# A gated four-branch block: branch gates computed ahead of the mixers' projections, as seven half-size products per pair of column blocks

## The chip, the core and the metric

The kernel runs on one core of a Trainium2 chip. The metric is the device time of one execution in microseconds (us); a kernel's time is the median of its runs.

## The reference, cut to what matters

One layer, T = 1024 tokens, D = 1024 channels, all in float32. The part that the change concerns:

```python
h = rms_norm(x, norm_mix_g) * (1 + sc1) + sh1
p = h @ w_in                                   # mixers' columns, then 4 * D gate columns
y_a, y_b, y_c, y_d = rwkv7(...), spatial_gating(...), short_conv(...), s5(...)
# each mixer ends with  o @ w_out : 256 -> 1024; s5 has a second, sigmoid half
gates = sigmoid(p[..., OFF_G:]).reshape(T, 4, D)
merged = gates[0] * y_a + gates[1] * y_b + gates[2] * y_c + gates[3] * y_d
x = x + gt1 * (merged @ w_o)
h2 = rms_norm(x, norm_ffn_g) * (1 + sc2) + sh2
x = x + gt2 * (square(relu(h2 @ ffn_w1)) @ ffn_w2)
return rms_norm(x, final_g)
```

## The kernel before, in words

Every float32 operand of a large product is split into a rounded high part (`hi`, type fp32r, a cast on ACT) and a remainder (`lo`, a subtraction on DVE); both stand in `split`, lines 72 and 73. One product of a 128-row piece is three matmuls, hi·hi, hi·lo and lo·hi, into one PSUM bank (`mm3`, line 112). Each call of `mm3` is a **beat**: it also lets a background generator advance (`step`), which puts the small work of the S5, spatial-gating and RWKV mixers between the large products, after a given number of beats. RWKV is in three parts: `rwkv_1` prepares chunks, `rwkv_2` solves 32-row triangular blocks on DVE alone (lines 1051 and 1053), and `rwkv_3` is a serial recurrence over chunks on PE, ACT and DVE. `mods` sums the conditioning vector's products on DVE (lines 310 and 312) in the same background.

Activations are kept transposed: `hh[k]` and `hl[k]`, k = 0..7, are 128 channels by 1024 tokens. The order of the large work is: a, b and conv columns of `w_in`, then `gates(br)` for the branches 3 (S5), 1, 2 and 0 (RWKV), then `w_o`, then the feed-forward part. `gates(br)` runs over eight column blocks j and two token halves hf. For each it makes the gate, 8 beats over the 8 channel blocks (`h_mm`), then the mixer's projection, 2 beats (4 for S5); ACT takes the sigmoid out of PSUM (L1222), DVE multiplies projection and gate (L1236), POOL adds into `merged` (L1239, L1233 for S5); for the last branch DVE adds (L1241) and splits the sum for `w_o` (L72, L73). Weights come from `weight_queue`: `take` keeps `depth` = 2 prepared operands ahead, tiles `raw`, `whi` and `wlo` with two buffers each. Loads, stores and their waits stand in one SP queue, in order. The tile framework's scheduler then orders each engine's instructions, so that rows of neighbouring steps interleave.

```python
for hf in range(2):
    pg = self.h_mm(w, hf)
    nc.scalar.activation(sg, pg, AF.Sigmoid)
    ...
    v.tensor_tensor(m if first else sg, py[0], sg, op=ALU.mult)
```

Names: `pmm` are four PSUM banks for large products; `m`, `n`, `ev`, `sig`, `g2` (shown as `g`) are float32 tiles of 128x512; `wyr`, `wyh`, `wyl` are a projection's weights raw and split; `MX` in DRAM holds the mixers' outputs. The feed-forward part's first product (`up_queue`, `ffn_up`) is already made in seven products instead of eight.

Of the kernel before, what the change touches and what calls it, by code (L numbers as in the profile page):

```python
# [10 lines left out]
F32 = mybir.dt.float32  # L11
# [29 lines left out]
class Kern:  # L41
# [49 lines left out]

    def behind_next(self):

        es = ExitStack()
        if self.ahead:
            w = self.ahead[0]
            for ins in self.tail[id((w[0] if len(w) == 3 else w)[0])]:
                es.enter_context(self.tc.issue_after(ins))
        return es
# [755 lines left out]
    def conv(self):  # L855
# [322 lines left out]

    def wy_load(self, br, name, j):
# [18 lines left out]
        return w, hi, lo

    def gates(self, br, first, last):  # L1200

        nc, v = self.nc, self.nc.vector
        glu = br == 3
        ne = 2 if glu else 1
        if not first:
            self.flush()
        mx = [[None] * 2 for _ in range(2)]
        for hf in range(2):
            for r in range(2):
                raw = self.ev()  # L1210
                nc.sync.dma_start(raw, self.MX[br, r, :, hf * HALF : hf * HALF + HALF])
                hi, lo = self.g(dt=F32R, tag="n"), self.g(dt=F32R, tag="n")
                self.split(hi, lo, raw)
                mx[hf][r] = (hi, lo)
        for j in range(8):
            w, wyh, wyl = self.take()
            for hf in range(2):
                pg = self.h_mm(w, hf)
                sg = self.sg()
                pin = self.behind_next if hf else ExitStack  # L1220
                with pin():
                    nc.scalar.activation(sg, pg, AF.Sigmoid)  # L1222
# [458 lines left out]
    def weight_queue(self):  # L1681
# [206 lines left out]
```

## Time and profile before

| what | value |
|---|---|
| median of 3 runs | 1697.05 us (1696.71 to 1697.99) |
| the profiled execution's own time | 1698.43 us |
| its span, first to last instruction | 1696.7 us |
| granted TensorE clock, mean | 0.987 |
| PE busy / DVE / ACT / POOL | 1613.8 / 1004.0 / 652.4 / 631.0 us |
| moved by DMA | 234.68 MB, 138 GB/s over the span |

PE is the matmul engine, DVE the vector engine, ACT the scalar engine, POOL GpSimd, SP the queue that issues most DMAs. Busy time is the union of an engine's instructions; matmuls overlap in the record, so their durations (about 400 ns) are not their pace. An instruction's duration includes what it waits for inside the engine. L numbers are lines of the kernel before.

### The profile page before, as it was taken

Reading aid. Unit: us, or ns where it says so; the run is one execution under the profiler, and the core shown is the slowest. Engines: PE = TensorE matmul, PEld = TensorE weight load, DVE = VectorE, ACT = ScalarE, POOL = GpSimd, SP = SyncE. Lnnn points to the kernel's source line nnn. Section 1 sums busy time; section 2 is a strip of 40 time slices with the busy share of each in tenths; the row PEclk is TensorE's granted clock in tenths of the full one; section 3 lists DMA queues with packets and bytes.
Section 4 is the critical chain, followed back from the end, with each engine's and each line's share of the span. In section 5 each row is a group of like instructions: output and inputs, shape, how many; then the busy total and the mean of one; then the engine's idle time right before and its main releaser. Section 6 shows DMA issues by size and latency. Waiting matters only on the chain.

```text
span 1696.7 us, 22664 instructions
## 1 busy us (share of the span) xinstructions
PE 1613.8 (95%) x8083; PEld 1293.7 (76%) x8083; DVE 1004.0 (59%) x1729; ACT 652.4 (38%) x1206; POOL 631.0 (37%) x505
## 2 busy tenths in 40 slices
PE   3999999999999999999999998799999999999996
PEld 2798778777777777777888876588888878888875
DVE  5673545666538824233433567865555469669986
ACT  4522124556522112211222245544455446444343
POOL 2260223112220223222101374576556565128662
PEclk9999999999999999999999999799999999999998
DMA  8423136777675345331211446354444485562332
GB/s 276 131 63 66 52 118 195 180 188 175 143 151 182 63 138 174 107 116 35 75 48 62 170 146 172 92 178 150 154 157 141 161 309 170 161 223 87 99 125 99
DMA packets 262723, 234.68 MB, mean 138 GB/s; under 512 B 79351, under 2 KB 194282, under 8 KB 262610
## 3 DMA queue, kind: packets, MB, share of 16 engines
q1 hardware_dynamic: 254002, 224.83, 44.2%
q10 hardware_dynamic: 8464, 8.01, 1.9%
q8 instruction: 64, 1.05, 0.3%
q0 software_dynamic: 144, 0.39, 0.1%
q14 instruction: 49, 0.40, 0.1%
HBM read 172.59 MB, written 60.58 MB: 137 GB/s over the span
## 4 chain that ended last, share of the span: by engine, by line
PE 37%; DVE 8%; DMA 2%; issue 2%; ACT 2%; POOL 1%; POOLq 0%; DVEq 0%; ACTq 0%; SPq 0%
PE pmm L112 22%; PE pax L112 8%; PE pch L112 7%; DVE g L73 2%; DVE xx L73 1%; DMA raw<-in_ffn_w_dram 1%; DVE m L1523 1%; DMA raw<-FA 1%; DMA w<-in_ffn_w_dram 1%; ACT g L72 1%; DVE wlo L73 0%; POOL ev L1513 0%; DVE m L1526 0%; DVE m L1328 0%; DVE n L73 0%
## 5 line engine op out<-in xcount | busy, mean ns | idle before, releaser
L112 PE MATMUL pmm<-hh,whi 128*128 128x512 f32 x704 | 285.3, 407 | 3.9 <-ACT hh L410 3.9
L112 PE MATMUL pmm<-hl,whi 128*128 128x512 f32 x704 | 278.7, 396 | 5.3 <-POOL hl L412 4.1
L112 PE MATMUL pmm<-hh,wlo 128*128 128x512 f32 x704 | 278.3, 395 | 0.0
L73 DVE TENSOR_TENSOR wlo<-raw,whi 128x512 fp32r<-128x512 f32 (+1 forms) x140 | 105.8, 793 | 129.4 <-ACT whi L72 126.1
L112 PEld LDWEIGHTS pmm<-hh,whi 128*128 128x128 f32 x704 | 132.6, 189 | 34.7 <-ACT hh L410 5.1
L112 PEld LDWEIGHTS pmm<-hl,whi 128*128 128x128 f32 x704 | 133.2, 189 | 33.6 <-POOL hl L412 4.5
L112 PEld LDWEIGHTS pmm<-hh,wlo 128*128 128x128 f32 x704 | 133.2, 189 | 29.7 <-issue 0.9
L72 ACT CAST whi<-raw 128x512 fp32r<-128x512 f32 (+1 forms) x140 | 79.0, 612 | 158.2 <-PE pmm L112 141.5
L112 PE MATMUL pmm<-g,g 128*128 128x512 f32 x456 | 107.3, 390 | 0.6 <-DVE xx L1425 0.6
L112 PE MATMUL pmm<-n,wyh 128*128 128x512 f32 x320 | 106.3, 411 | 0.8 <-ACT n L72 0.8
L73 DVE TENSOR_TENSOR g<-raw,g 128x512 fp32r<-128x512 f32 x75 | 72.0, 959 | 48.7 <-ACT g L72 42.6
L112 PEld LDWEIGHTS pmm<-g,g 128*128 128x128 f32 x456 | 85.6, 188 | 18.9 <-DVE xx L1425 1.0
L1239 POOL TENSOR_TENSOR m<-m,sig 128x512 f32<-128x512 f32 x32 | 45.1, 1409 | 129.9 <-DVE sig L1236 129.8
L1222 ACT ACTIVATE sig<-pmm 128x512 f32<-128x512 f32 x64 | 38.1, 596 | 142.6 <-PE pmm L112 131.4
L84 POOL TENSOR_TENSOR raw<-raw,gt 128x1024 f32<-128x1024 f32 x16 | 39.1, 2444 | 136.3 <-DMA raw<-in_w_o_dram 131.6
L112 PE MATMUL pmm<-g,m 128*128 128x512 f32 x256 | 82.5, 404 | 3.4 <-ACT m L72 3.4
L1236 DVE TENSOR_TENSOR sig<-pmm,sig 128x512 f32<-128x512 f32 x48 | 32.9, 686 | 69.0 <-PE pmm L112 68.9
L72 ACT CAST g<-raw 128x512 fp32r<-128x512 f32 x75 | 46.5, 620 | 69.8 <-PE pmm L112 34.6
L112 PEld LDWEIGHTS pmm<-n,wyh 128*128 128x128 f32 x320 | 60.5, 193 | 16.4 <-issue 1.2
L73 DVE TENSOR_TENSOR n<-xx,m 128x512 fp32r<-128x512 f32 x64 | 54.9, 863 | 28.4 <-ACT m L72 28.3
L72 ACT CAST m<-xx 128x512 fp32r<-128x512 f32 x64 | 39.3, 620 | 75.8 <-PE pch L112 27.4
L112 PE MATMUL pch<-g,g 128*128 128x512 f32 x222 | 59.7, 402 | 8.7 <-DVE g L73 5.7
(480 smaller groups left out, 3833.3 us busy)
## 6 DMA issues: line engine op xcount, KB each, us to landing
raw<-FA SPq DMA_DIRECT2D x56, 512.0 KB
raw<-in_w_in_dram SPq DMA_DIRECT2D x52, 512.0 KB
FA<-xx SPq DMA_DIRECT2D x80, 256.0 KB
raw<-in_ffn_w_dram SPq DMA_DIRECT2D x36, 512.0 KB
mod<-in_ada_w_dram SPq DMA_DIRECT2D x64, 256.0 KB
w<-in_ffn_w_dram SPq DMA_DIRECT2D x32, 512.0 KB
raw<-in_w_o_dram SPq DMA_DIRECT2D x16, 512.0 KB
FA<-ev SPq DMA_DIRECT2D x32, 256.0 KB
```

Of the source, the lines that this page charges most:

```text
L72: a = nc.scalar.copy(hi, src)
L73: b = (eng or nc.vector).tensor_tensor(lo, src, hi.bitcast(F32), op=ALU.subtract)
L84: nc.gpsimd.tensor_tensor(raw, raw, scale, op=ALU.mult)
L112: mm = lambda *x, **y: self.nc.tensor.matmul(*x, **y, skip_group_check=open_)
L1222: nc.scalar.activation(sg, pg, AF.Sigmoid)
L1236: v.tensor_tensor(m if first else sg, py[0], sg, op=ALU.mult)
L1239: nc.gpsimd.tensor_tensor(m, m, sg, op=ALU.add)
L1523: v.tensor_tensor(dst, x, y, op=ALU.add)
```

## The change

The gates of all branches are made first, in `gates()`, for pairs of column blocks. A pair's 256 columns by 1024 channels, and h as 1024 channels by 1024 tokens, are cut in two by two, and the pair takes seven products of halves (4 beats each) instead of eight (Winograd's form of Strassen's scheme). `h_sums` and `h_blocks` make the three sums of h's quarters that the scheme needs, beside and behind the conv columns; `gate_queue` makes the weights' sums on POOL in place in the raw tiles and splits each operand; depth is 3. Products 1, 6, 7 and 4 of a pair accumulate in one bank, 5 and 3 in another; between them ACT copies a bank out or DVE adds the earlier copy to it. The sigmoids go to a DRAM tensor `G` (64 stores of 256 KB) and come back in `merge`, three column blocks ahead (64 loads). `merge(br)` then has only the projections (2 or 4 beats) and the elementwise merge; in the branches 1 and 2 DVE adds one half and POOL the other; in the last branch, 0, POOL adds both and DVE makes the remainders. The mixers' outputs are loaded (`mx_load`) into the tiles of h that are free by then.

```diff
-            self.conv()
+            sums = self.h_sums()
+            self.conv(lambda: next(sums, None))
...
+            self.depth = 3
+            self.h_blocks()
+            self.gates()
+            self.depth = 2
             self.merged = [[None] * 2 for _ in range(8)]
-            self.gates(3, True, False)
-            self.gates(1, False, False)
-            self.gates(2, False, False)
+            self.merge(3, 1)
+            self.merge(1, 2)
+            self.merge(2, None)
             for _ in self.bg:
                 pass
...
-            self.gates(0, False, True)
+            self.mx_load(0)
+            self.merge(0, None)
...
+    def gate_queue(self):
...
+        pairs = [(br, 2 * j) for br in (3, 1, 2, 0) for j in range(4)]
+        n = len(pairs)
+        seq = [(0, 1), (1, 1), (0, 2), (1, 2), (0, 5), (0, 6), (0, 3), (0, 7), (1, 5), (0, 4), (1, 6), (1, 3), (1, 7)]
+        for i in range(2, n):
+            seq += [(i, 1), (i - 1, 4), (i, 5), (i, 2), (i, 6), (i, 3), (i, 7)]
+        seq += [(n - 1, 4)]
...
+            hi, lo = (self.WY.tile([P, 4, P], F32R, tag="x", name=f"g{z}_{self.n}_{m}") for z in "hl")
+
+            self.split(hi, lo, {1: A(1, 1), 2: A(1, 2), 3: A(1, 2), 4: A(2, 2), 5: A(2, 1), 6: A(2, 1), 7: A(1, 1)}[k])
+            if k == 1:
+                gp.tensor_tensor(A(1, 1), A(1, 1), A(2, 1), op=ALU.subtract)
+                gp.tensor_tensor(A(2, 1), A(2, 1), A(2, 2), op=ALU.add)
+            elif k == 5:
+                gp.tensor_tensor(A(2, 1), A(2, 2), A(1, 1), op=ALU.subtract)
+            if (k == 5 and i < 2) or (k == 2 and i >= 2):
+                gp.tensor_tensor(A(1, 2), A(1, 2), A(2, 1), op=ALU.subtract)
...
+    def gates(self):
...
+        banks = [self.ps("mm") for _ in range(4)]
...
+        for i, k in self.gate_seq:
+            hi, lo = self.take()
+            pt = banks[{5: 2, 3: 2, 2: 3}.get(k, i % 2)]
+            for q in range(4):
+                self.mm3(pt, hi[:, q], lo[:, q], *B[k][q], q == 0 and k in (1, 5, 2), q == 3 and k in (4, 3, 2), open_=True)
...
+            else:
+                r, c = {2: (1, 1), 3: (1, 2), 7: (2, 2)}[k]
+                t = e[i] if k == 7 else p[i][:, int(k == 3)]
+                v.tensor_tensor(t, pt, t, op=ALU.add)
+                out(i, r, c, t)
...
+    def merge(self, br, nxt):
...
+                v.tensor_tensor(sg, py[0], sg, op=ALU.mult)
+                if not last:
+                    (v if hf else gp).tensor_tensor(m, m, sg, op=ALU.add)
+                else:
+                    gp.tensor_tensor(sg, m, sg, op=ALU.add)
+                    hi, lo = self.g(dt=F32R), self.g(dt=F32R, tag="g2")
+                    self.split(hi, lo, sg)
```

The order of instructions moves with it. **DVE while `rwkv_2` runs.** Before (`rpr`, `rti` are the solve; `wlo` and `wyl` are remainders of weights, `sig` gates):

```order
L1051 TENSOR_TENSOR rpr_4497<-rti_4377,rta_4376 128x676
L1053 TENSOR_REDUCE rti_4377<-rpr_4497 128x26
L1051 TENSOR_TENSOR rpr_4497<-rti_4377,rta_4376 128x729
L1053 TENSOR_REDUCE rti_4377<-rpr_4497 128x27
L1051 TENSOR_TENSOR rpr_4497<-rti_4377,rta_4376 128x784
L73 TENSOR_TENSOR wlo_5001<-raw_4998,whi_5000 128x512 x2
L73 TENSOR_TENSOR wyl_5009<-wyr_5006,wyh_5008 128x256
L1236 TENSOR_TENSOR sig_5081<-pmm_5083,sig_5081 128x512
L1053 TENSOR_REDUCE rti_4377<-rpr_4497 128x28
```

and in the changed kernel (line numbers are its own: 1044 and 1046 are the solve; `gl_56` is the remainder of the 57th product's weights, L1287 adds a bank to a copy):

```order
L73 TENSOR_TENSOR gl_56_5146<-whi_4814,gh_56_5145 128x512
L1044 TENSOR_TENSOR rpr_4621<-rti_4497,rta_4496 128x676
L1046 TENSOR_REDUCE rti_4497<-rpr_4621 128x26
L1287 TENSOR_TENSOR gp_5053<-pmm_3320,gp_5053 128x512
L73 TENSOR_TENSOR gl_57_5171<-whi_4986,gh_57_5170 128x512
L1044 TENSOR_TENSOR rpr_4621<-rti_4497,rta_4496 128x729
L1046 TENSOR_REDUCE rti_4497<-rpr_4621 128x27
L1287 TENSOR_TENSOR ev_5098<-pmm_3319,ev_5098 128x512
L73 TENSOR_TENSOR gl_58_5192<-raw_4984,gh_58_5191 128x512
L1044 TENSOR_TENSOR rpr_4621<-rti_4497,rta_4496 128x784
```

Each step of the solve now has a weights' remainder beside it, and often an addition out of PSUM. **DVE in the last branch.** Before, per token half of a column block: the product with the gate, the sum, its remainder:

```order
L73 TENSOR_TENSOR wyl_7495<-wyr_7491,wyh_7494 128x256
L1241 TENSOR_TENSOR sig_7563<-m_3493,sig_7563 128x512
L73 TENSOR_TENSOR g_1240_7575<-sig_7563,m_7574 128x512
L1236 TENSOR_TENSOR sig_7618<-pmm_7620,sig_7618 128x512
L1241 TENSOR_TENSOR sig_7618<-m_3625,sig_7618 128x512
L73 TENSOR_TENSOR g_1247_7630<-sig_7618,m_7629 128x512
```

and in the changed kernel (L1364 is the product with the gate; the sum is POOL's):

```order
L73 TENSOR_TENSOR wyl_8317<-wyr_8313,wyh_8316 128x256
L73 TENSOR_TENSOR g_1273_8396<-n_8367,m_8395 128x512
L1364 TENSOR_TENSOR n_8371<-pmm_8423,n_8371 128x512
L73 TENSOR_TENSOR g_1276_8409<-n_8369,m_8408 128x512
L1364 TENSOR_TENSOR n_8373<-pmm_8436,n_8373 128x512
L73 TENSOR_TENSOR wyl_8383<-wyr_8379,wyh_8382 128x256
L73 TENSOR_TENSOR g_1282_8433<-n_8371,m_8432 128x512
```

The remainder of a half now stands behind the next half's product with the gate, and waits for POOL's sum. **POOL at the end of that branch**, in the changed kernel (L1368 are the sums, L84 scales `w_o`'s raw weights; before, L84 had no sums beside it):

```order
L1368 TENSOR_TENSOR n_8488<-m_7774,n_8488 128x512
L84 TENSOR_TENSOR raw_8564<-raw_8564,gt_8345 128x1024
L1368 TENSOR_TENSOR n_8523<-m_7799,n_8523 128x512
L1368 TENSOR_TENSOR n_8525<-m_7818,n_8525 128x512
L84 TENSOR_TENSOR raw_8599<-raw_8599,gt_8345 128x1024
```

The first piece of `w_o` is scaled between the sums of the last column blocks.

## Rows read from the trace of the kernel before

**Rows 1.** The page: busy time by engine, and slices of the span

```profile
PE 1613.8 (95%) x8083; PEld 1293.7 (76%) x8083; DVE 1004.0 (59%) x1729; ACT 652.4 (38%) x1206; POOL 631.0 (37%) x505
...
PE   3999999999999999999999998799999999999996
```

**Rows 2.** Windows: stretch, its length, busy us per engine, PEclk, DMA share, GB/s

```profile
260.00:355.00 95.00, 92.94 (x483) 74.68 (x483) 64.72 (x143) 42.93 (x81) 25.96 (x42) 1.00 0.71 189
...
515.00:582.00 67.00, 62.76 (x261) 49.22 (x260) 65.97 (x106) 14.93 (x29) 10.98 (x7) 0.97 0.44 134
...
637.00:815.00 178.00, 176.66 (x1384) 130.74 (x1385) 64.53 (x196) 39.11 (x94) 49.29 (x54) 1.00 0.37 108
815.00:934.00 119.00, 119.00 (x520) 97.43 (x519) 48.05 (x76) 33.29 (x62) 10.27 (x5) 1.00 0.19 57
934.00:960.00 26.00, 26.00 (x115) 21.25 (x114) 14.44 (x16) 6.27 (x12) 9.94 (x4) 1.00 0.48 162
1100.00:1200.00 100.00, 99.99 (x432) 80.77 (x431) 56.53 (x76) 47.74 (x82) 68.77 (x48) 1.00 0.50 166
```

**Rows 3.** One line (L1222): sigmoids from PSUM, in 829:927, then 360:830

```profile
L1222 ACT ACTIVATE sig<-pmm x15: 589/599/599, 829.6 to 926.1; 128x512 f32<-128x512 f32 x15
...
L1222 ACT ACTIVATE sig<-pmm x49: 587/597/602, 360.9 to 829.6; 128x512 f32<-128x512 f32 x49
```

**Rows 4.** Waits of PE in 285:582: total us, times, longest

```profile
PE pax L142 <- DVE macc L312: 4.2, 2, 2.9
PE pch L142 <- DVE rar L981: 2.1, 2, 1.2
PE pch L142 <- DVE rt L937: 1.7, 1, 1.7
```

**Rows 5.** Groups of DVE in 515:582: busy, mean ns, idle before

```profile
L1051 DVE TENSOR_TENSOR rpr<-rti,rta 128x1 f32<-128x1 f32 (+30 forms) x31 | 25.7, 828 | 0.5
L1053 DVE TENSOR_REDUCE rti<-rpr 128x1 f32<-128x1 f32 (+30 forms) x31 | 15.4, 496 | 0.5
L312 DVE SCALAR_TENSOR_TENSOR macc<-mod,cact,macc 128x512 f32<-128x512 f32 x14 | 11.0, 788 | 0.0
L73 DVE TENSOR_TENSOR wlo<-raw,whi 128x512 fp32r<-128x512 f32 x9 | 7.0, 803 | 0.0
```

**Rows 6.** Groups of DVE in 830:934, the last branch

```profile
L73 DVE TENSOR_TENSOR g<-sig,m 128x512 fp32r<-128x512 f32 x15 | 10.4, 692 | 10.3 <-ACT m L72 10.3
L73 DVE TENSOR_TENSOR wlo<-raw,whi 128x512 fp32r<-128x512 f32 x16 | 10.3, 688 | 24.1 <-ACT whi L72 21.0 <-PE pmm L112 3.1
L1241 DVE TENSOR_TENSOR sig<-m,sig 128x512 f32<-128x512 f32 x15 | 10.3, 689 | 0.3
L1236 DVE TENSOR_TENSOR sig<-pmm,sig 128x512 f32<-128x512 f32 x15 | 10.3, 687 | 30.0 <-PE pmm L112 30.0
L73 DVE TENSOR_TENSOR wyl<-wyr,wyh 128x256 fp32r<-128x256 f32 x6 | 2.5, 415 | 0.0
```

**Rows 7.** Groups of DVE, then of POOL, in 934:960, the start of w_o

```profile
L73 DVE TENSOR_TENSOR wlo<-raw,whi 128x512 fp32r<-128x512 f32 x9 | 10.6, 1209 | 12.4 <-ACT whi L72 9.3 <-PE pmm L112 3.1
L1276 DVE TENSOR_TENSOR n<-pmm,n 128x512 f32<-128x512 f32 x4 | 2.8, 689 | 1.6 <-PE pmm L112 0.9 <-DMA raw<-in_w_o_dram 0.7
...
L84 POOL TENSOR_TENSOR raw<-raw,gt 128x1024 f32<-128x1024 f32 x4 | 9.9, 2496 | 22.9 <-DMA raw<-in_w_o_dram 22.9
```

**Rows 8.** Groups of POOL in 637:815: the merge's sums

```profile
L1239 POOL TENSOR_TENSOR m<-m,sig 128x512 f32<-128x512 f32 x18 | 24.2, 1347 | 51.4 <-DVE sig L1236 51.3
```

**Rows 9.** The page: groups of ACT, the casts of weights and the sigmoids

```profile
L72 ACT CAST whi<-raw 128x512 fp32r<-128x512 f32 (+1 forms) x140 | 79.0, 612 | 158.2 <-PE pmm L112 141.5
...
L1222 ACT ACTIVATE sig<-pmm 128x512 f32<-128x512 f32 x64 | 38.1, 596 | 142.6 <-PE pmm L112 131.4
```

More of the change, by code (lines that the diff above doesn't have):

```diff
@@ L90, in wload @@
         return hi, lo
[L92 to L99, printed above, removed]
     def take(self):
@@ L853, in sgu, with conv @@
             yield
-    def conv(self):
+    def conv(self, between):
         nc, v = self.nc, self.nc.vector
@@ L863, in conv @@
                 pt = self.h_mm(w, hf)
+                between()
                 cg.append(self.g(tag="n"))
@@ L870, in conv @@
                 pt = self.h_mm(w, hf)
+                between()
                 v.tensor_tensor(z[hf][:, 2:], pt, cg[hf], op=ALU.mult)
@@ L1194, in wy_load, with mx_load @@
                 nc.sync.dma_start(wy[:, :, e], wsrc[:, :, e, cc])
-        hi = self.WY.tile([P, 2, ne, P], F32R, tag="hi", name=f"wyh_{self.n}")
-        lo = self.WY.tile([P, 2, ne, P], F32R, tag="lo", name=f"wyl_{self.n}")
+        hi = self.W.tile([P, 2, ne, P], F32R, tag="whi", name=f"wyh_{self.n}")
+        lo = self.W.tile([P, 2, ne, P], F32R, tag="wlo", name=f"wyl_{self.n}")
         self.split(hi, lo, wy)
[L1198 to L1207, printed above, removed]
+        return hi, lo
+    def mx_load(self, br):
+        self.flush()
+        self.mx = [[None] * 2 for _ in range(2)]
+        tags = [z + str(4 * (br in (1, 0)) + k) for z in (("hh",) if br in (3, 1) else ("hl",)) for k in range(4)]
         for hf in range(2):
@@ L1210, in gates, with g_load @@
                 raw = self.ev()
[L1211 to L1214, printed above, removed]
+                self.nc.sync.dma_start(raw, self.MX[br, r, :, hf * HALF : hf * HALF + HALF])
+                self.n += 1
+                y = self.H.tile([P, 2, HALF], F32R, tag=tags.pop(0), name=f"mx_{self.n}")
+                self.split(y[:, 0], y[:, 1], raw)
+                self.mx[hf][r] = (y[:, 0], y[:, 1])
+    def merge(self, br, nxt):
+        nc, v, gp = self.nc, self.nc.vector, self.nc.gpsimd
+        first, last = br == 3, br == 0
+        ne = 2 if first else 1
+        mx = self.mx
+        if nxt is not None:
+            self.mx_load(nxt)
+        gt = {}
+        def g_load(j):
+            for hf in range(2):
+                gt[j, hf] = self.g(tag="n")
+                nc.sync.dma_start(gt[j, hf], self.G[br, j, hf])
+        for j in range(3):
+            g_load(j)
         for j in range(8):
-            w, wyh, wyl = self.take()
+            wyh, wyl = self.take()
             for hf in range(2):
[L1218 to L1222, printed above, removed]
                 py = []
@@ L1805, in background @@
                 e5.close()
[L1806 removed]
+                self.WY = pool(e1, "wy", 8, **left)
                 self.bg2 = self.mods(pool(em, "mods", 1, **right))
```

110 lines of the change are left out of this document (93 added, 17 removed).

## The prediction

> **What bounds the kernel now.** I read the page first. PE is busy 95% of the span and nearly every slice reads 9 [rows 1]: work taken from PE counts in full, as long as nothing else becomes late. The windows over the gate stage (gates and projections of all branches, about 355 to 934 us) say the same stretch by stage: in the last branch, where no background is left, PE has no idle time at all, 119.00 of 119 us [rows 2]. DVE is the next engine: 65.97 of 67 us while `rwkv_2` solves, but a third of the time in the last stretches. The sigmoids out of PSUM are a clock for PE, since each stands 10 beats behind the one before: 15 of them in 96.5 us [rows 3] are 14 x 10 beats x 3 matmuls, **0.2298 us a matmul**, 0.689 us a beat. The first 49 sigmoids take 468.7 us for 512 beats [rows 3], of which the large matmuls are 353.0; so 116 us are background matmuls on PE and its waits. Waits alone are small: the three largest in 297 us sum to 8.0 us [rows 4].
>
> **What goes.** Before, 64 gates of 8 beats are 1536 matmuls; now 16 pairs of 7 products of 4 beats are 1344. 192 x 0.2298 = **44.1 us** less. The projections keep their 480 matmuls, the background its own. All of the 44.1 us lie on the path, as PE is the bound.
>
> **What comes, part by part.** Products first.
> - Each product needs a cast (0.612 us, ACT) and a remainder (0.688, DVE); per pair come three copies out of PSUM and four sigmoids on ACT (0.596 each) and three additions from PSUM on DVE (0.687) [rows 6, 9]. Per pair: ACT 7 x 1.208 = 8.5 us, DVE 6.9, against 28 beats = 19.3 us on PE. That is hidden, where the background leaves room.
> - POOL: four sums of 128x512 per pair, 4 x 1.347 = 5.4 us [rows 8]; hidden, but beside DVE (below).
> - h's sums and blocks: 36 DVE instructions of about 0.69 us, 25 us, and 12 on POOL, 16 us, near the conv columns. DVE is busy 64.72 of 95 us there [rows 2], so 30 us are free, and the first four products need none of these blocks (4 x 4 beats = 11 us). It just fits: bounds 0 (all in the gaps) and 10 us (a third of it in the way); I take 3.
> - While `rwkv_2` runs: the solve (25.7 + 15.4 us) and the conditioning sums (11.0) are 52 us of DVE [rows 5] in 67 us. Of these 67 some 10 are background on PE, so that 57 / 0.689 = 82 beats go by. In the changed kernel 82 beats are 20.5 products: 20.5 x 0.72 + 8.8 x 0.69 = 21 us, with the background 73 us of DVE, over PE's 67 by 6; by 11, if each of some 12 POOL sums beside them stretches a neighbour by 0.4 us (1.209 - 0.688 = 0.52 in [rows 6, 7]). Operands lie up to three products (8 us) ahead, which covers a part. Bounds 0 and 11; I take 6.
> - Background matmuls that wait for DVE: 8.0 us now [rows 4]. With more ahead of it in DVE's queue, bounds 0 and 16 more (each wait tripled); I take 4. For `rwkv_3`, whose stretch has DVE at 64.53 of 178 us [rows 2], 1.
> - DRAM: 64 stores and 64 loads of 256 KB, 34 MB. A store goes 5 beats behind its sigmoid's place, and a pair's weights are asked for 7 products (19 us) before their use, so a late sigmoid in SP's queue has room. I cost them at nothing; without that cover it is rival C.
>
> Then the merge, where the cover is thin. A column block of the branches 1, 2 and 0 is now 4 beats = 2.76 us of PE, before 20 beats.
> - Branches 1 and 2, DVE per block: two products with gates, the weights' remainder, one sum: 2 x 0.687 + 0.415 + 0.689 = 2.48 us [rows 6], under PE's 2.76. But POOL's sum of the other half (1.347) runs beside them. What that does shows in one pair of rows: the same remainder `wlo` takes 688 ns where POOL is nearly idle [rows 6] and **1209 ns** beside POOL's scaling [rows 7], while a product out of PSUM stays at 689 [rows 7]. With both SBUF-to-SBUF pieces stretched so, the block is 1.37 + (0.415 + 0.689) x 1.76 = 3.31 us. Bounds for 16 blocks: 0 and 16 x 0.55 = 8.8; POOL runs half of the time, I take 4.
> - Last branch, per half (PE 1.38 us): product 0.687, half a weights' remainder 0.21, remainder of the sum. Unstretched 0.692, together 1.59; beside POOL, which now makes every sum, 1.209, together **2.10 us**. 16 halves: 25.4 or 33.7 us, against PE's 22.1. Bounds +3.3 and +11.6. I take the upper one, because POOL's sums fill 1.347 of each half, more than the scaling did there (9.94 of 26 us [rows 2]).
> - Start of `w_o`: its first piece now stands behind the sums, on POOL (2.5 us [rows 7]) and on DVE. Bounds 0 and 5; I take 2. Before there was no gap, PE went on without idle time (26.00 of 26) [rows 2].
> The mixers' outputs for the last branch are not late: in the order the background ends within the first merge, over 60 beats before they are needed.
>
> **The sum:** -44.1 + 3 + 6 + 4 + 1 + 4 + 11.6 + 2 = -12.5 us. The profiled execution took 1698.43 us, 1.4 over the median, so 1685.9 for it and **about 1685 us** for the median of runs.
>
> A rule of the Trainium skill speaks against this change at the merge: "SBUF — State Buffer", section "Who interferes with whom", has it that a DVE instruction with two SBUF inputs and a GpSimd instruction that reads SBUF exclude each other for the whole instruction, and that one with at most one SBUF input is free. The 1209 against 688 ns agrees with it, and so does the product out of PSUM at 689. By it the two would not stretch each other by 1.76 but take turns, and the sum would be that of rival B, 1693, instead of 1685.
>
> **The rivals.**
> - **A: the other engines fit.** For it speaks the feed-forward product, already in seven: PE 99.99 of 100 us with POOL at 68.77 and DVE at 56.53 [rows 2]. Then the solve's overrun is mostly covered (2), background waits cost 2, the first merges nothing, the last branch its lower bound: -44.1 + 2 + 2 + 3.3 + 2 = -34.8, 1662 us. Against it: there a product has 2.76 us for one remainder, in the last branch a half has 1.38 us for 1.59.
> - **B: DVE and POOL take turns** (the rule just named). Last branch: 1.347 (POOL) + 0.692 + 0.21 = 2.25 us a half, 13.9 over PE; first merges: product 0.687, sum on POOL 1.347 with the second product beside it, then 0.415 + 0.689, 3.14 us a block, 6.1 over; the solve 10; the rest as above: -44.1 + 3 + 10 + 4 + 1 + 6.1 + 13.9 + 2 = -4.1, 1693 us.
> - **C: the way through DRAM.** A merge block loads 512 KB of gates and 128 KB of weights in 2.76 us, 237 GB/s. The conv stretch moved 189 GB/s at a DMA share of 0.71, the start of `w_o` 162 at 0.48 [rows 2]; in proportion 266 and 337 at the full share, so it fits. If only 200 GB/s come through, a block takes 3.28 us, 24 blocks 12.5 us more than the forecast: 1697 us, no change.
> - **D, slower: PSUM hand-overs.** One bank takes the products 1, 6, 7 and 4 of a pair. Between 6 and 7, and between 7 and 4, stands one other product, 2.76 us, in which ACT's copy or DVE's addition must be done. There are 32 such hand-overs. It decides as soon as the eviction comes over 2.76 us late in the mean: each 0.5 us more costs 16 us. On DVE a solve step (0.83 + 0.50 in the mean, about 3 us for the longest), a remainder and a conditioning sum may stand ahead of it, some 3.5 us: 32 x 0.7 = 22 us more, 1706 us. Against it: the evictions stand early in the order, and the long steps last only three pairs.
> That fewer matmuls are issued than claimed is no rival: the order holds 7 x 12 for each pair.
>
> **How the numbers follow.** Forecast 0.36, with its own range 1676 to 1694; A 0.20; B 0.20; C 0.08; D 0.16. About 0.2%, 3.4 us, is what a measurement can tell from no change. Faster beyond that: nearly all of the forecast (0.34), A, half of B (it lies on the edge): 0.64. Within: the rest of B and of the forecast and most of C: 0.18. Slower: D and a little of C: 0.18. The range reaches from A to D, 1661 to 1706; left out is what lies beyond either end, under 2 in 10.
>
> **What would show it.** Right: `L1287` and the sigmoids keep up, so that in the gate stage PE waits sum to some 10 us above before; in the last merge DVE (with POOL over 80% busy) is the bound and its remainders read 1.0 to 1.4 us instead of 0.69; PE idle just ahead of `w_o`, and most of what is lost lies in the merges. A shows as PE without idle time through the last merge; B as remainders near 0.69 + 1.35 or POOL sums stretched by the same, and idle time in all three short merges; C as DVE waiting for `G` loads; D as PE's products 7 and 4 waiting for ACT's copy and DVE's addition in many pairs. The forecast is wrong if the last branch ends within 4 us of PE's pace, or if the seven products themselves stall PE by over 25 us.

## The result and the profile after

The changed kernel takes **1740.48 us** (median of 4 runs, 1737.48 to 1743.75); the kernel before, beside it on the same chip, 1697.52 (4 runs, 1696.71 to 1699.78). The ratio is 1.0251, with a 95% interval of 1.0230 to 1.0273: 43 us slower. Forecast were 1685 us and a range of 1661 to 1706, so that both sign and range were wrong. The profiled execution took 1741.21 us, its span is 1739.5. Over the study the median of the kernel before, run beside each group of kernels, lay between 1697.5 and 1700.7 us; so kernels are compared by their ratios to it too.

The page of the changed kernel, busy time and the slices that answer to [rows 1]:

```profile
PE 1602.0 (92%) x7891; PEld 1269.3 (73%) x7891; DVE 1121.2 (64%) x1861; ACT 715.7 (41%) x1316; POOL 751.4 (43%) x581
...
PE   3999997989988999999999899699999999999997
...
PEclk9999998999998999999999999899999999999998
```

PE has 192 matmuls less and only 11.8 us less busy time, at a longer span. The slices 7 to 13 (about 260 to 565 us) and 23 (start of `w_o`) no longer read 9 throughout, and PEclk falls in some of them. The windows by stage (columns: busy us of PE, PEld, DVE, ACT, POOL, then granted clock, share and rate of the DMA) say where; they answer to [rows 2]:

```profile
272.00:290.00 18.00, 9.26 (x34) 7.55 (x34) 12.57 (x26) 0.53 (x1) 15.66 (x19) 0.63 0.17 64
...
374.00:614.50 240.50, 208.14 (x889) 156.83 (x887) 165.59 (x275) 109.51 (x190) 71.60 (x54) 0.93 0.63 166
614.50:834.00 219.50, 211.82 (x1521) 157.90 (x1522) 97.77 (x224) 77.47 (x154) 64.28 (x62) 0.99 0.51 157
...
892.00:936.00 44.00, 44.00 (x196) 36.31 (x194) 40.54 (x60) 7.01 (x17) 20.71 (x16) 1.00 0.72 211
936.00:969.00 33.00, 24.66 (x96) 16.64 (x94) 27.24 (x37) 10.16 (x20) 21.62 (x15) 1.00 0.60 186
969.00:998.00 29.00, 26.35 (x96) 20.25 (x97) 19.31 (x19) 7.70 (x14) 18.22 (x9) 0.88 0.37 118
```

Three places lose: a stretch of 18 us in the conv columns in which PE works for 9 and POOL for nearly 16; the first half of the gates, where PE's busy time is 32 us under the span and the clock 0.93; and the last merge (936 to 969) with the start of `w_o` behind it. The merges of the branches 1 and 2 (892 to 936) run with PE never idle.

**The conv columns.** The timeline (start, duration, engine, line, operation; idle time ahead of it and its releaser in brackets). L1183 to L1186 are `h_sums`, L1197 is a sum of `h_blocks`, and L828 is the spatial-gating mixer's last small step on POOL, an addition:

```profile
272.90 1.80 POOL L1197 TENSOR_TENSOR m<-m,m 128x512 f32<-128x512 f32 x1
...
272.91 0.66 DVE L1185 TENSOR_TENSOR m<-m,hh 128x512 f32<-128x512 f32 x1
...
274.66 1.28 POOL L1183 TENSOR_TENSOR m<-hh,hl 128x512 f32<-128x512 f32 x1
...
275.90 1.26 POOL L1184 TENSOR_TENSOR m<-hh,hl 128x512 f32<-128x512 f32 x1
275.97 1.73 DVE L1185 TENSOR_TENSOR m<-m,hh 128x512 f32<-128x512 f32 x1 [2.35 <-POOL m L1183]
...
278.09 1.26 POOL L1183 TENSOR_TENSOR m<-hh,hl 128x512 f32<-128x512 f32 x1
...
279.31 1.31 POOL L1184 TENSOR_TENSOR m<-hh,hl 128x512 f32<-128x512 f32 x1
...
281.71 1.70 POOL L1197 TENSOR_TENSOR m<-m,m 128x512 f32<-128x512 f32 x1
...
283.37 1.17 POOL L828 TENSOR_TENSOR m<-m,lnb 128x256 f32<-128x256 f32 x1
...
284.59 1.97 PE L133 MATMUL pax<-m,wst 128*128 128x64 f32 x8 [8.74 <-POOL m L828]
```

PE's next instruction is a background matmul that needs L828. POOL works in the order of its queue, and six sums of h stand ahead of L828 in these rows, two of them (L1197) sums that no product needs before the gates. PE waits 8.74 us at one instruction. Where the two engines overlap in these rows, one of them is longer: at 275.97 DVE's L1185 takes 1.73 us, with POOL's sum beside it at 1.26; the same instruction took 0.66 at 272.91, and there POOL's sum beside it took 1.80.

**The gates' first half.** PE's waits (us in total, times, the longest), to be read beside [rows 4]:

```profile
PE pax L133 <- DVE macc L303: 8.5, 5, 3.7
PE pmm L103 <- ACT gh L72: 7.0, 3, 3.5
PE pch L133 <- DVE rbk L976: 4.4, 1, 4.4
...
PE pmm L103 <- DVE ev L1287: 2.0, 1, 2.0
```

Groups of DVE and POOL in the same stretch (L303 are the conditioning sums, L73 remainders, L1287 adds a bank to a copy; L1243 to L1248 are the weights' sums):

```profile
L303 DVE SCALAR_TENSOR_TENSOR macc<-mod,cact,macc 128x512 f32<-128x512 f32 x41 | 33.1, 808 | 4.6 <-DMA mod<-in_ada_w_dram 4.6
L73 DVE TENSOR_TENSOR gl<-whi,gh 128x512 fp32r<-128x512 f32 x25 | 21.2, 847 | 9.7 <-ACT gh L72 9.5
L73 DVE TENSOR_TENSOR gl<-raw,gh 128x512 fp32r<-128x512 f32 x30 | 21.1, 704 | 7.7 <-ACT gh L72 5.4 <-PE pmm L103 2.1
L1287 DVE TENSOR_TENSOR gp<-pmm,gp 128x512 f32<-128x512 f32 x16 | 11.0, 689 | 16.4 <-PE pmm L103 15.7 <-issue 0.6
```

```profile
L1246 POOL TENSOR_TENSOR whi<-whi,raw 128x512 f32<-128x512 f32 x9 | 17.2, 1909 | 31.5 <-DVE gl L73 31.5
...
L1244 POOL TENSOR_TENSOR whi<-whi 128x512 f32<-128x512 f32 x8 | 12.6, 1578 | 0.6
```

POOL's sum of 512 columns takes 1.58 to 1.91 us here, by the groups of its four lines (two of them shown), against 1.347 in [rows 8]. Of DVE's remainders those of `gl<-whi` take 847 ns and those of `gl<-raw` 704, where [rows 6] have 688 to 692; the addition out of PSUM (689 ns) is as there. The conditioning sums (808 ns) are no longer than in the kernel before, where they took 832 in 355:582.

**The clock.** Behind a long wait PE doesn't go on at its pace. PE's rows at the wait of 4.44 us, then two windows, just behind it and later:

```profile
386.93 2.53 PE L133 MATMUL pch<-rar,rbk 64*128 64x128 f32 x16 [4.44 <-DVE rbk L976]
...
389.98 0.63 PE L103 MATMUL pmm<-hl,gh 128*128 128x512 f32 x1
...
390.40 0.63 PE L103 MATMUL pmm<-hh,gl 128*128 128x512 f32 x1
...
394.76 0.39 PE L103 MATMUL pmm<-hl,gh 128*128 128x512 f32 x1
...
394.98 0.40 PE L103 MATMUL pmm<-hh,gl 128*128 128x512 f32 x1
```

```profile
387.00:394.00 7.00, 7.00 (x31) 5.94 (x32) 3.45 (x6) 2.67 (x4) 0.00 (x0) 0.54 0.35 110
395.00:400.00 5.00, 5.00 (x23) 3.93 (x21) 3.92 (x8) 3.73 (x9) 0.00 (x0) 1.00 0.53 105
```

At 389.98 and 390.40 two matmuls of 512 columns start 0.42 us apart, at 394.76 and 394.98 0.22. The granted clock of the 7 us in between is 0.54, that is, nearly all of it at the lower level, 1.2 of 2.4 GHz. So the wait of 4.44 us cost an estimated 3.2 us more (7 x 0.46). The longest wait of [rows 4] is 2.9 us. From 271 us (conv columns) to the end of the first 383 matmuls of `w_o` the granted clock is at the lower level in 13 stretches, in which PE works for 55.9 us; in the kernel before it is there in three, with 10.2 us. Ahead of each of the 13 PE had waited.

**The last merge**, the groups that answer to [rows 6, 7]:

```profile
L1368 POOL TENSOR_TENSOR n<-m,n 128x512 f32<-128x512 f32 x12 | 18.1, 1520 | 8.4 <-DVE n L1364 5.8 <-issue 2.6
...
L73 DVE TENSOR_TENSOR g<-n,m 128x512 fp32r<-128x512 f32 x12 | 12.1, 1010 | 5.8 <-ACT m L72 5.8
...
L1364 DVE TENSOR_TENSOR n<-pmm,n 128x512 f32<-128x512 f32 x12 | 8.1, 678 | 0.0
```

Remainders take 1010 ns beside sums of 1520 ns on POOL, products out of PSUM 678. The 96 matmuls take 33.5 us from the first to the first of `w_o`, 2.10 us a half in the mean; the last 2.7 of them are PE's wait for the cast of `w_o`'s first weights. Neither engine is full: in 936:969 DVE works for 27.24 and POOL for 21.62 of 33 us. The rows of a column block say why:

```profile
958.02 1.09 DVE L73 TENSOR_TENSOR g<-n,m 128x512 fp32r<-128x512 f32 x1 [1.24 <-ACT m L72]
...
959.37 0.68 DVE L1364 TENSOR_TENSOR n<-pmm,n 128x512 f32<-128x512 f32 x1
...
960.20 2.85 POOL L1368 TENSOR_TENSOR n<-m,n 128x512 f32<-128x512 f32 x2 [1.63 <-DVE n L1364]
...
961.85 0.62 ACT L72 CAST m<-n 128x512 fp32r<-128x512 f32 x1 [2.63 <-POOL n L1368]
...
962.50 1.09 DVE L73 TENSOR_TENSOR g<-n,m 128x512 fp32r<-128x512 f32 x1 [1.25 <-ACT m L72]
```

Remainder, then the next block's product on DVE, its sum on POOL, its cast on ACT, its remainder: a ring over three engines that takes 4.48 us a block, 2.24 a half. Each waits for the one before it, DVE for 1.25 us and POOL for 1.63. The first six halves still go at 1.43 us, near PE's pace (935.76 to 944.35).

### The profile page after: what moved, and what is told of

Its sections match the earlier page's. It is cut to its first block, busy times and chain, and to the rows that moved or that the text cites. A ratio compares the mean times of both kernels' runs of the same rounds, so it can differ in the third digit from the quotient of the medians.

```text
span 1739.5 us, 23035 instructions
## 1 busy us (share of the span) xinstructions
PE 1602.0 (92%) x7891; PEld 1269.3 (73%) x7891; DVE 1121.2 (64%) x1861; ACT 715.7 (41%) x1316; POOL 751.4 (43%) x581
## 4 chain that ended last, share of the span: by engine, by line
PE 32%; DVE 9%; issue 3%; DMA 2%; POOL 2%; ACT 2%; SPq 0%; POOLq 0%; DVEq 0%; ACTq 0%
PE pmm L103 18%; PE pax L103 7%; PE pch L103 7%; DVE g L73 2%; DVE xx L73 1%; DVE wlo L73 1%; DMA w<-in_ffn_w_dram 1%; DMA raw<-FA 1%; DVE m L1652 1%; POOL n L1368 1%; DMA raw<-in_ffn_w_dram 0%; POOL ev L1642 0%; ACT g L72 0%; DVE n L73 0%; DVE m L1655 0%
## 5 line engine op out<-in xcount | busy, mean ns | idle before, releaser
L103 PE MATMUL pmm<-hh,gh 128*128 128x512 f32 x256 | 108.7, 425 | 8.9 <-ACT gh L72 8.9
L103 PE MATMUL pmm<-hh,gl 128*128 128x512 f32 x256 | 106.5, 416 | 2.6 <-DVE gl L73 2.6
L103 PE MATMUL pmm<-hl,gh 128*128 128x512 f32 x256 | 106.2, 415 | 0.0
L73 DVE TENSOR_TENSOR g<-raw,g 128x512 fp32r<-128x512 f32 x75 | 71.8, 957 | 49.2 <-ACT g L72 43.1
L73 DVE TENSOR_TENSOR wlo<-raw,whi 128x512 fp32r<-128x512 f32 (+1 forms) x76 | 59.6, 819 | 67.7 <-ACT whi L72 67.7
L103 PE MATMUL pmm<-mx,wyh 128*128 128x512 f32 x320 | 101.2, 397 | 2.2 <-ACT wyh L72 2.2
L103 PE MATMUL pmm<-m,gh 128*128 128x512 f32 x256 | 84.1, 407 | 2.0 <-DVE ev L1287 2.0
L103 PE MATMUL pmm<-hh,whi 128*128 128x512 f32 x192 | 81.0, 428 | 3.8 <-ACT hh L401 3.8
L103 PE MATMUL pmm<-hl,whi 128*128 128x512 f32 x192 | 78.6, 410 | 5.7 <-POOL hl L403 4.0
L103 PE MATMUL pmm<-hh,wlo 128*128 128x512 f32 x192 | 77.7, 405 | 0.0
L73 DVE TENSOR_TENSOR n<-xx,m 128x512 fp32r<-128x512 f32 x64 | 56.2, 882 | 28.5 <-ACT m L72 28.5
L1243 POOL TENSOR_TENSOR raw<-raw,whi 128x512 f32<-128x512 f32 x16 | 24.8, 1552 | 110.9 <-DVE gl L73 88.3
L103 PEld LDWEIGHTS pmm<-mx,wyh 128*128 128x128 f32 x320 | 58.8, 188 | 15.9 <-ACT wyh L72 3.5
L73 DVE TENSOR_TENSOR gl<-raw,gh 128x512 fp32r<-128x512 f32 x64 | 45.9, 718 | 33.9 <-ACT gh L72 29.4
L103 PEld LDWEIGHTS pmm<-hh,gh 128*128 128x128 f32 x256 | 50.3, 196 | 23.6 <-ACT gh L72 10.7
```

Of the source, the lines that this page charges most:

```text
L73: b = (eng or nc.vector).tensor_tensor(lo, src, hi.bitcast(F32), op=ALU.subtract)
L103: mm = lambda *x, **y: self.nc.tensor.matmul(*x, **y, skip_group_check=open_)
L1243: gp.tensor_tensor(A(1, 1), A(1, 1), A(2, 1), op=ALU.subtract)
```

## The experiments

Each kernel was timed in three rounds with the kernel before beside it. The table has the ratio to it with its 95% interval, and, from the profile of each, the time between the first matmuls of the stages: the conv columns (the last 264 of their 288 matmuls of 512 columns), gates with merges, of these the merges, and the first 383 matmuls of `w_o`. Over all 288 the conv columns take 93.3 us before, 113.4 in the changed kernel and 97.5 in e2. The conv stretch of the same code reads 101.4 to 107.0 us in six of these profiles (changed, e3, e4, e6, e7, e13), so that a few us there mean nothing. e8, e10 to e12 and e14 build on one another.

| kernel | median us | ratio (interval) | conv | gates + merges | merges | w_o |
|---|---|---|---|---|---|---|
| before | 1697.5 | 1 | 85.2 | 579.4 | | 95.5 |
| changed | 1740.5 | 1.0251 (1.0230 to 1.0273) | 101.9 | 595.1 | 135.5 | 103.8 |
| e1 eight products | 1715.8 | 1.0098 (1.0083 to 1.0113) | 85.3 | 590.4 | 120.8 | 103.0 |
| e2 no blocks of h | 1719.1 | 1.0116 (1.0099 to 1.0134) | 89.4 | 586.7 | 136.4 | 103.3 |
| e3 no weights' sums | 1714.4 | 1.0086 (1.0071 to 1.0101) | 101.4 | 567.0 | 135.5 | 103.6 |
| e4 weights' sums on DVE | 1719.0 | 1.0109 (1.0089 to 1.0129) | 104.5 | 570.8 | 136.0 | 103.6 |
| e5 all sums on DVE | 1717.3 | 1.0100 (1.0079 to 1.0122) | 98.2 | 577.1 | 135.5 | 104.3 |
| e6 last merge without sum | 1732.5 | 1.0190 (1.0158 to 1.0221) | 107.0 | 584.6 | 127.6 | 100.6 |
| e7 mixed merges alone | 1737.7 | 1.0218 (1.0196 to 1.0240) | 102.2 | 590.0 | 131.1 | 103.1 |
| e8 e5 and e7 | 1711.1 | 1.0063 (1.0043 to 1.0083) | 96.2 | 575.0 | 130.3 | 103.2 |
| e9 no sums at all | 1693.9 | 0.9968 (0.9955 to 0.9980) | 87.2 | 565.2 | 136.6 | 103.7 |
| e10 e8, late sigmoids | 1706.5 | 1.0048 (1.0029 to 1.0067) | 97.0 | 566.5 | 128.9 | 103.1 |
| e11 e8, late sums of h | 1705.8 | 1.0044 (1.0027 to 1.0061) | 95.7 | 569.8 | 131.4 | 102.7 |
| e12 e10, e11, depth 4 | 1690.1 | 0.9954 (0.9937 to 0.9971) | 95.7 | 552.8 | 130.4 | 102.7 |
| e13 depth 4 alone | 1730.0 | 1.0165 (1.0138 to 1.0192) | 103.7 | 578.7 | 136.9 | 105.4 |
| e14 e12, weights' sums on POOL | 1712.3 | 1.0065 (1.0050 to 1.0080) | 98.8 | 572.7 | 130.8 | 102.6 |

**e1, eight products in the new order.**

```diff
-        q += self.gate_queue()
+        for br in (3, 1, 2, 0):
+            for j in range(8):
+                blk(OFF_G + br * D + j * P)
```

with `gates` a loop of `h_mm`, sigmoid and store, and no `h_sums` or `h_blocks`.

> The gates in eight plain products again (192 matmuls of 0.2298 us more, 44.1 us), with no sums of h or of weights and no hand-overs, but still ahead of the projections, with sigmoids through DRAM and the merges behind. Theory 1 (the seven products themselves stall PE: operands, sums, copies): only the merges' cost, some 16 to 20 us, stands against the kernel before: 1713 to 1720 us, faster than the changed kernel. Theory 2 (the new order, the way through DRAM and the merges cost the time, as the prediction had most of it): the whole loss stays and the 44 us come on top, 1770 to 1785 us. A start of the first merge that waits for its mixer's loads, some 4 us, is part of this edit.

1715.8 us: theory 1. The kernel with 44.1 us more of matmuls is 25 us faster than the changed one. Its conv columns are those of before; what it loses is the last merge (its 96 matmuls take 33.5 us here too) and `w_o`, 103.0 for 95.5. Moving the gates and sending the sigmoids through DRAM costs nothing else that shows: gates with merges are 11.0 us longer than before, the last merge alone 11.6.

**e2, e3, e9: parts of the seven products left out.**

```diff
-            sums = self.h_sums()
-            self.conv(lambda: next(sums, None))
...
+            self.conv(lambda: None)
...
-            self.h_blocks()
...
-        B = {1: ..., 4: self.g4, 5: of_h(0, h1), 6: self.g2, 7: self.g3}
+        B = {1: ..., 4: of_h(4, h0), 5: of_h(0, h1), 6: of_h(0, h1), 7: of_h(4, h1)}
```

> The sums and blocks of h are left out (the products 4, 6 and 7 take plain quarters of h, so the gates are not the reference's); all matmuls and all else stay. Theory 1a (what the sums put into POOL's and DVE's queues during the conv columns holds up the background's matmuls): the stretch from the b columns to the first gate is 20 us shorter, and the first pairs gain another 5: 1715 to 1720 us. Rival (the stretch is longer because its clock is lower, whatever is in the queues, or because POOL is held by something else): 1735 us or more.

1719.1 us; the conv stretch is 12.5 us shorter, the gates with their merges 8.4. The wait for L828 is gone: from 262 to 360 us PE's longest wait is 1.2 us. Theory 1a.

e3 removes the weights' sums in `operand`:

```diff
-                gp.tensor_tensor(A(1, 1), A(1, 1), A(2, 1), op=ALU.subtract)
-                gp.tensor_tensor(A(2, 1), A(2, 1), A(2, 2), op=ALU.add)
-                gp.tensor_tensor(A(2, 1), A(2, 2), A(1, 1), op=ALU.subtract)
-                gp.tensor_tensor(A(1, 2), A(1, 2), A(2, 1), op=ALU.subtract)
```

> The four sums of weights per pair on POOL are left out (the operands are plain weights; the gates are not the reference's); matmuls, casts, remainders and copies stay. Theory 1b (POOL's sums and DVE's work on SBUF keep each other waiting, and late sums make late operands): about half of the gate stage's 45 us goes, 1715 to 1722 us. Rival (PSUM hand-overs and the longer queue of remainders on DVE): within 6 us of the changed kernel, 1734 or more.

1714.4 us: all of it in the gates, 595.1 to 567.0. Theory 1b.

e9 has the edits of e2 and e3:

> The changed kernel without the sums and blocks of h and without the sums of weights (e2 and e3 together; the gates are not the reference's): seven products with their casts, remainders, copies out of PSUM and the merges. If the two costs are apart, their 21.5 and 26 us add up: 1690 to 1696 us. If they are one (DVE's and POOL's load in the first pairs), 1704 or more. Against e1 it also shows what hand-overs and remainders leave of the 44.1 us: at 1693, 23 us of them.

1693.9 us, 46.6 under the changed kernel, for 21.4 and 26.1 in e2 and e3: the two costs lie apart and add up. Here the gates alone take 565.2 - 136.6 = 428.6 us, against 590.4 - 120.8 = 469.6 in e1: **41.0 of the 44.1 us** that the seven products save are there, with all their casts, remainders, copies out of PSUM and additions. In the changed kernel it is 469.6 - 459.6 = 10.0. The sums alone eat the rest.

**e4, e5: the sums on DVE.**

```diff
-                gp.tensor_tensor(A(1, 1), A(1, 1), A(2, 1), op=ALU.subtract)
+                v.tensor_tensor(A(1, 1), A(1, 1), A(2, 1), op=ALU.subtract)
```

(all four in `operand`; e5 also the sums of h).

> The same four sums per pair on DVE instead of POOL, 64 x 0.69 = 44 us more of DVE work, 86 us less on POOL. Theory 1b (a POOL sum holds DVE up for most of its 1.35 us): DVE loses less by making the sum itself, and the operands come earlier: 10 to 20 us faster than the changed kernel, 1720 to 1730. Rival (DVE's load is what is short): 15 to 30 us slower, 1755 to 1770.

1719.0 us, theory 1b: with 64 instructions more for the busier engine the kernel is 21 us faster. DVE's groups and PE's waits in the first half of its gates:

```profile
L303 DVE SCALAR_TENSOR_TENSOR macc<-mod,cact,macc 128x512 f32<-128x512 f32 x41 | 30.4, 742 | 5.3 <-DMA mod<-in_ada_w_dram 5.3
...
L73 DVE TENSOR_TENSOR gl<-whi,gh 128x512 fp32r<-128x512 f32 x25 | 17.6, 703 | 0.6 <-ACT gh L72 0.4
L1287 DVE TENSOR_TENSOR gp<-pmm,gp 128x512 f32<-128x512 f32 x16 | 10.9, 684 | 15.8 <-PE pmm L103 14.8 <-issue 1.0
...
L1246 DVE TENSOR_TENSOR whi<-whi,raw 128x512 f32<-128x512 f32 x8 | 5.4, 679 | 0.0
```

```profile
PE pmm L103 <- ACT gh L72: 6.6, 3, 3.5
...
PE pax L133 <- DVE macc L303: 2.3, 3, 1.3
PE pch L133 <- DVE rbk L976: 1.2, 1, 1.2
```

The conditioning sums fall from 808 to 742 ns, the remainders of `gl<-whi` from 847 to 703, a step of the RWKV mixer (L930) from 546 to 482; the remainders of `gl<-raw` do not (704, here 720). A weights' sum takes 679 ns on DVE. Over the 269 DVE instructions that both stretches have in common the changed kernel spends 16.6 us more (mean durations by line and shape, from the trace), and e4's 32 sums cost 22.3. So DVE's busy time hardly moves, 165.4 us in the changed kernel and 163.0 in e4 (4.7 us of the solve lie in the first stretch and not in the second), while POOL's sums are gone. PE's waits for `macc` go from 8.5 to 2.3 us and those for `rbk` from 4.4 to 1.2. Those for casts (`gh`) stay.

> As e4, and the twelve sums of h on DVE as well, so that nothing of the seven products is left on POOL. Theory 1a as the trace shows it (in the changed kernel POOL has seven sums of 512 columns ahead of the small multiplication that the spatial-gating mixer's matmuls wait for, one wait of 8.7 us): that wait goes, and the conv stretch shortens by 8 to 13 us, 1706 to 1711 us. Rival (DVE's load of 12 x 0.69 = 8.3 us more takes the place of POOL's): within 4 us of e4, 1715 to 1723.

1717.3 us: the rival. The conv stretch is 6 us shorter than in e4, little beyond the spread of the same code, and the gates are 6 longer. PE still waits 3.7 us for L828, instead of 8.7: now sums of h stand among the mixer's steps on DVE, at 270.11, 271.56 and 272.20 between its L822 (269.78) and its L826 (273.32). A place in a queue ahead of the background's steps costs there too.

**e6, e7, e8: the merges.**

```diff
-                    gp.tensor_tensor(sg, m, sg, op=ALU.add)
```

> The changed kernel without POOL's 16 sums in the last merge: the product alone is split for w_o, so that the output is not the reference's. Theory (the last merge's cost is POOL's sum beside DVE's remainder, 33.5 us for 96 matmuls that need 21.9): DVE then needs 0.69 + 0.69 + 0.21 = 1.59 us a half, the stage 25.4 us, 8 us less, and w_o starts with 3 us less to wait for: 1728 to 1733 us. Rival (the stage is held by ACT's casts or the loads of the gates): within 3 us of the changed kernel.

1732.5 us. The stage is 25.1 us long, for an expected 25.4. But 2.9 of them are PE's wait for `w_o`'s first weights, which stays; the 96 matmuls have no wait among them and take 22.2 us, PE's pace, so that the expected number was met by luck. The remainders are short again:

```profile
L73 DVE TENSOR_TENSOR g<-n,m 128x512 fp32r<-128x512 f32 x12 | 7.9, 683 | 0.1
```

e7 mixes the blocks, with all mixers' outputs held in the 16 tiles of h, and half of the last branch's sums on DVE:

```diff
+BLOCKS = (
+    [(j, br) for j in range(4) for br in (3, 1, 2)],
+    [x for s in range(4, 8) for x in ((s, 3), (s, 1), (s, 2), (2 * s - 8, 0), (2 * s - 7, 0))])
```

> The changed kernel, with the blocks of the merges in another order: for column blocks 0 to 3 the branches 3, 1, 2 in turn, then for each of 4 to 7 the branches 3, 1, 2 and two blocks of branch 0, so that the last branch's remainders stand beside the S5 blocks, where PE has twice the work. Theory (an average over the four merges fits PE, the last one by itself doesn't): the 11.6 us of the last merge and some 7 us at the start of w_o go, 1720 to 1728 us. Rival (POOL and DVE keep each other up in any order): within 4 us of the changed kernel, 1736 or more.

1737.7 us, close to the rival: the merges gain 4.4 us, not 11.6, and `w_o` starts no better. That start is therefore not explained by the last merge's sums alone: e6 gave 3.2 of the 8.3 us back, e7 0.7, and the wait of 2.7 us ahead of them stays in e6. A reason that fits but was not tried: `take` prepares two operands ahead, which were 40 beats in the kernel before and are 8 beats now. In the traces the first load of `w_o`'s weights is issued 9.7 us before its first matmul (959.57 for 969.29), and 40.8 us before it in the kernel before (893.28 for 934.11); their scaling starts 3 us before it, and 24 in the kernel before.

> e5 and e7 together: all sums of the seven products on DVE, and the merges' blocks mixed. If the two causes are apart, their gains add up: e5's 30 us and e7's 16 us off 1740, 1690 to 1697 us, about the kernel before. If they are the same time counted twice, 1702 or more.

1711.1 us, in the second of the two ranges. That does not show the same time counted twice: the ranges were set from expected gains that were too large, and the measured ones add up (23.2 and 2.8 us apart, 29.4 together).

**e10, e11, e12: what is left in the gates.** ACT's list of waits in e8 showed the sigmoids of added banks waiting 12.4 us for DVE between 470 and 550 us, with casts queued behind. e10 keeps such a sigmoid back until the next product's matmuls are issued; e11 calls `between()` in the second half of `conv` only:

```diff
+            if src is None:
+                late.append(sig)
...
+            for sig in due:
+                sig()
```

```diff
-                between()
+                if r:
+                    between()
```

> e8, with the sigmoid of a bank that DVE adds to issued one product later. Theory (ACT works in order: a sigmoid that waits for DVE's addition, which waits for PE, holds up the casts of the next products; in e8's first half PE waits 6.6 us for casts and 3.4 for remainders, and runs at the lower clock after the longest): 5 to 9 us faster than e8, 1702 to 1706. Rival (the casts are late because the sums of weights in place come late on DVE): within 3 us of e8.

> e8, with the sums of h begun only in the second half of the conv columns, when the spatial-gating mixer is done. Theory (in the conv stretch the sums stand ahead of the background's small steps, whichever engine makes them): the stretch falls from 96 to about 89 us, the first products lose 2 of it: 1704 to 1708. Rival (the sums are then late for the fifth product): within 3 us of e8 or slower.

1706.5 and 1705.8 us; both intervals overlap e8's, so that each alone is only likely to help. In e11 the reason given was wrong: the conv stretch stays (95.7 for 96.2), the 5 us are in the gates.

e12 takes both, and depth 4 with ten tiles `x` instead of eight and one buffer of RWKV's `t` less:

```diff
-                self.WY = pool(e1, "wy", 8, **left)
+                self.WY = pool(e1, "wy", 10, **left)
-                self._r_bufs = {"t": 15, "pin": 4, "am": 2, "st": 2}
+                self._r_bufs = {"t": 14, "pin": 4, "am": 2, "st": 2}
-            self.depth = 3
+            self.depth = 4
```

> e10 and e11 together, with four operands prepared ahead instead of three (one buffer of the RWKV mixer's less, to make room). If lateness of operands is what is left in the gates, 1690 to 1699 us, at or under the kernel before; if it is DVE's load while the RWKV solve runs, depth gives nothing, and the time is that of e10 and e11 added up, 1700 to 1704.

**1690.1 us, ratio 0.9954** (0.9937 to 0.9971): faster than the kernel before by 8 us, than the changed one by some 50. Its gates alone take 422.4 us.

**e13, e14: depth against POOL.** e13 is the changed kernel with the diff of e12 just shown; e14 is e12 with the diff of e4 undone.

> The changed kernel, all sums on POOL as it has them, with four operands ahead instead of three (and one buffer of the RWKV mixer's less): nothing else. Theory L (operands are merely late by a product or so; POOL's sums only add to that): depth covers most of the gate stage's loss, 1715 to 1722 us. Theory P (beside POOL's sums DVE's own work is lengthened, so that DVE falls behind by more than depth can cover, and the conv stretch isn't touched): 1728 to 1738.

> e12, with the weights' four sums per pair back on POOL: late sigmoids, late sums of h and four operands ahead stay. Theory L: within 5 us of e12, 1688 to 1695, since depth covers what POOL takes longer. Theory P: most of the 21 us between the changed kernel and e4 comes back, 1702 to 1712.

1730.0 and 1712.3 us: theory P at both ends (the second lies at its edge). Depth gives the changed kernel 10 to 15 us (by medians and by ratios); POOL's sums cost 19 us even with it (1.0065 against 0.9954). PE's waits in the first half of the gates, in e13, e14 and e12 (line numbers shifted by 5 to 7 in the last two):

```profile
PE pax L133 <- DVE macc L303: 7.1, 4, 3.8
PE pch L133 <- DVE rbk L976: 5.2, 2, 4.9
...
PE pmm L103 <- ACT gh L72: 2.7, 2, 2.0
```

```profile
PE pax L138 <- DVE macc L308: 7.7, 2, 6.1
PE pch L138 <- DVE rbk L983: 4.9, 1, 4.9
...
PE pmm L108 <- ACT gh L77: 2.0, 1, 2.0
```

```profile
...
PE pch L138 <- DVE rbk L983: 2.8, 3, 1.4
...
PE pax L138 <- DVE macc L308: 0.7, 1, 0.7
```

Depth covers the products' own operands (`gh` 7.0 to 2.7 or 2.0 us). It can't cover the background's matmuls, which stand in PE's order and wait for DVE: `macc` and `rbk` stay at 12 to 13 us together while POOL makes the sums, and are 3.5 when it doesn't.

## Why the prediction was wrong, point by point

- **192 matmuls, 44.1 us off the path:** right. e9 has 41.0 of them.
- **"POOL: four sums ... hidden, but beside DVE (below)":** the step that failed most. Below, only some 12 of the 64 sums were costed, at 0.4 us each, and only while `rwkv_2` solves. Beside them DVE's work on SBUF takes longer than in e4, the background's small steps included, and PE waits for these in order. The background's steps were about as long before (conditioning sums 832 ns, the RWKV step 529, in 355:582), but DVE had 23 remainders of the gates' weights among them there, and 55 in the changed kernel's first half of the gates. e3 puts the price of POOL's sums at 26 us; e4 gets 21 back by moving them.
- **"h's sums and blocks ... it just fits", 3 us, at most 10:** e2 puts it at 21.4 us, 12.5 of them in the conv stretch of the table. I compared DVE's busy time with the free time of the stretch. What decides is whose turn it is: sums of h stood ahead of a 256-column addition that PE's next instruction needed.
- **"Background matmuls that wait for DVE", 4 us, at most 16:** right as a mechanism, too small. `macc` and `rbk` alone are 12.9 us in the first half of the gates, against 4.2 for `macc` in [rows 4], where `rbk` is not among the three largest.
- **No term for the clock:** long waits were followed by stretches at the lower level, as shown above. There PE works for 55.9 us, against 10.2 before; as a matmul starts about every 0.42 us there instead of 0.22, half of the difference, 23 us, is an upper estimate of what the clock takes, about half of the loss. It goes with the waits, and so is contained in the prices of e2 and e3: in gates and merges PE's time at the lower level is 35.4 us in the changed kernel, 12.8 in e3, 16.8 in e4, 11.3 in e9 and 6.0 in e12, for 10.2 before.
- **`rwkv_2`, 6 us; `rwkv_3`, 1; DRAM, 0:** the first and the last about right, the second too small. From 534 to 614 us, the RWKV solve among it, PE is idle for 10.8 us (80 - 69.17 by the windows), against 4.2 in 515:582 of [rows 2]; in the second half of the gates for 7.7 (219.50 - 211.82), against 1.3 in 637:815.
- **Last merge, 11.6 us; first merges 4:** right in number and over. 33.5 against 21.9 us for 96 matmuls is 11.6, by the 2.10 us a half that were worked out. That POOL's sums are the cause is shown (e6), but the number is luck: 2.7 of the 11.6 us are the wait for `w_o`'s weights, so that the merge itself costs 8.9. The forecast summed DVE's work with a remainder of 1.21 us, and was to be known by a POOL over 80% busy. The remainder takes 1.01, POOL works for 66% of the stretch, and the pace is that of the ring shown above, behind six faster halves. The branches 1 and 2 cost nothing (21.8 us each). In the S5 merge, costed at nothing, PE is idle for 1.7 us.
- **Start of `w_o`, 2 us, at most 5:** 8.3 in the table, and 11.0 with the 2.7 us of wait just named. Partly open: the late load of its first weights (see e7) fits and was not tried.
- **Rivals.** A held neither for the last branch nor for the gates. B named the right pair of engines, but at the merges. There the last one settles at 2.24 us a half for its 2.25, though by the ring and not by its sum of POOL's, DVE's and the weights' shares, and the first ones have none of its 6.1 us. C is excluded by e1 and by the two merges at PE's pace. D, the hand-overs, the only rival that was slower than before, is not what happened: PE's waits for `gp` and `ev` are 2.7 and 2.0 us in the first half of the gates, and e9 keeps every hand-over and loses only 3.1 of the 44.1 us.

The rule of the Trainium skill that the prediction set against the merge ("SBUF — State Buffer", section "Who interferes with whom": a DVE instruction with two SBUF inputs and a GpSimd instruction that reads SBUF exclude each other, one SBUF input is free) bears on the gates as much as on the merge. The runs agree in kind: remainders of `gl<-whi` 847 and 703 ns with and without POOL's sums, additions out of PSUM 689 and 684; the remainders of `gl<-raw`, 704 and 720, show nothing of it. How much of the 21 us is the lengthening of DVE's steps, and how much the longer sums (1.58 to 1.91 us for 0.68) in the chain of in-place operands, no run here separates.

What stays open besides: the conv stretch is still 10 us over before in e12, with DVE's sums in it.

## What to carry to other kernels

An operand that costs two reads of SBUF is not free on POOL because POOL is idle: beside a DVE that works on SBUF it can be cheaper to give the sum to the busier engine. Before a step is costed at nothing, look at what is queued behind it on its engine and whether PE's next instruction needs that, rather than at the stretch's busy share. And price a new wait on PE with the lower clock that can follow it, at the wait worked out here some 0.7 of its length again. Where work on one engine waits for a second and that for a third, count the ring and not only the busiest engine.

## What the runs showed of the hardware that was not expected

- A wait of 4.44 us on PE was followed by about 7 us at a granted clock of 0.54; the same matmuls then start 0.42 instead of 0.22 to 0.23 us apart.
- POOL's sum of 128x512 took 1.26 to 1.31 us in the conv columns at best and 1.91 in the mean of one line in the gates, where DVE worked for 165.59 of 240.5 us; the same sum on DVE 0.68.
- Adding 22.3 us of sums to DVE left its busy time in the stretch nearly as it was (165.4 and 163.0 us), since the stretch's other instructions (269 compared) became 16.6 us shorter without POOL's sums.
